# Probabilities by values in bursts of four steps instead of step by step, in a streaming encoder step with sparse attention

## Chip, cores and metric

The kernel runs on one core of a Trainium2 chip. The metric is the time of one execution on the device in microseconds (us), the median of several runs. TensorE (PE) multiplies matrices and transposes, VectorE (DVE) and ScalarE (ACT) work on vectors and empty PSUM, GpSimd (POOL) works on vectors in SBUF, and SyncE (SP) issues the DMAs.

## What is computed

One layer of a hybrid encoder over 2048 prompt tokens (with 16 meta tokens ahead of them) and 128 sample tokens. After one large input projection there are two branches, gated linear attention and sparse attention, each with its own output projection; the two are merged and projected once more. The change touches the sparse attention of the prompt: an indexer picks 256 admissible keys for each query, and 16 query heads of width 64 (4 groups of keys and values) attend over those.

```python
logits = jnp.einsum('bqgrd,bqkgd->bqgrk', qg, k_sel.astype(jnp.float32)) * DSA_SCALE
logits = jnp.where(keep[:, :, None, None, :], logits, -jnp.inf)
p = jax.nn.softmax(logits, axis=-1)
o = jnp.einsum('bqgrk,bqkgd->bqgrd', p, v_sel.astype(jnp.float32))
return o.reshape(bsz, nq, DSA_Q).astype(q.dtype)
```

The kernel does not gather: it multiplies the queries by all earlier keys and adds a mask of 0 or a very large negative number.

## The kernel before

Phase 1 makes all projections and the selection masks. Phase 2 holds the prompt's attention, with the sample tile and the linear attention as side work in its first part (query blocks 15 down to 8), and the projection `gla_project` (tile `pd`) beside it in its second (blocks 7 to 0). Phase 3 is `finish`: merge, output projection and final norm.

`attend(j)` (L998) handles a block of 128 queries against the key blocks 0 to j. It goes over two halves (8 heads each), two values of `k` (0 and 2), and two sides (two key groups). For each side:

- `logits` (L1092) loads two query heads, multiplies them by the keys into PSUM tiles `pl` (L1105, L1106; three buffers), adds the mask and takes the maximum on VectorE (L1107), reduces it (L1109), and takes the exponential on ScalarE (`act`, L154) into `lgl` and `lgu`.
- `probs` (L1040) transposes these probabilities, two key blocks of two heads per step: four transposes of 128x128 into one PSUM tile `px` (L1046; two buffers in the first part of phase 2, three in the second), and one copy to SBUF on ScalarE (L1054) or VectorE (L1056). Side 0 gives tiles `st0`, `st2`, ..., one buffer each; side 1 gives tiles `pt` from a pool of seven.
- `pv` (L1059), on side 1, multiplies a step's `st` and `pt` by the values into the PSUM tile `oo` (L1066): for each key block one product of `st` into partitions 0 to 63 and one of `pt` into partitions 64 to 127. Each is 64 columns of weights and 256 moving columns, in float32, and the trace holds two instructions for each.

The last two steps (`DEFER`) of a pair of sides wait in `self.due` and are put among the next pair's side 0 steps. The products of eight heads end with `finish_half`: the gate (`gate`, four transposes into `pl`), the meta rows (`pv_meta`: four transposes into `px`, one product into `oo`, L1077), one multiplication, and two DMAs.

The order within each engine is not the order of the code. A scheduler places instructions by their priority, the order of emission, among those that are ready in its own model of time. `early(n)` (L132) lowers the priority number by n, so that the instructions go ahead of some n earlier ones. The order is fixed when the program is built; the chip runs each engine's list in that order.

Of the kernel before, what the change touches and what calls it, by code (L numbers as in the profile page):

```python
# [37 lines left out]
NEG = -3.0e38  # L38
# [17 lines left out]
DEFER = 2  # L56
# [13 lines left out]
# Token tiles ("m" meta rows, "s" sample rows, else a prompt block) in pieces, two to a group of the  # L70
# projections; COL is a tile's first column in the scratch tensors.
# [17 lines left out]
def segments(n, most=512):  # L89
    """n split into even pieces of nearly equal width, none wider than a bank."""  # L90
    c = max(1, -(-n // most))
    w = -(-n // c)
    w += w % 2
    out, a = [], 0
    while a < n:
        out.append((a, min(w, n - a)))
        a += w
    return out


def level_masks():
    """1 where a key meets a query in the products of a chunk's levels: of a key with itself and with the
    other query of its pair; in groups of four blocks of 2, 8 and 32 tokens, of blocks 1 to 3 with the one
    before, of 2 and 3 with block 0, of 3 with block 1; the same of samples, two blocks of 8 each."""
    j = np.arange(P)[:, None]
    out = [j == np.arange(P)[None, :], j == 2 * np.arange(64)[None, :]]
    for s, blocks in (2, (0, 1, 2, 0, 0, 1)), (8, (0, 1, 2, 0, 0, 1)), (32, (0, 1, 2, 0, 0, 1)), (8, (0, -1, 2)):
        group = np.arange(P // (4 * s)).repeat(len(blocks) * s)[None, :]
        block = np.tile(np.repeat(blocks, s), P // (4 * s))[None, :]
        out.append((j // (4 * s) == group) & (j // s % 4 == block))  # L110
    return np.concatenate(out, 1).astype(np.float32)
# [6 lines left out]
class Trunk:  # L118
# [5 lines left out]
    # ---------------------------------------------------------------- helpers  # L124
    @contextmanager
    def later(self, n):
        """Instructions that yield to those of the next n or so."""
# [6 lines left out]
    def early(self, n):  # L134
        """Instructions that go ahead of the last n or so."""
# [23 lines left out]
    def split(self, hi, lo, src, scale=None):  # L159
        """src = hi + lo exactly; hi and lo are float32r."""  # L160
# [7 lines left out]
    def move(self, out, a):  # L168
        """A plain copy of float32r data."""
        self.nc.sync.dma_start(out.bitcast(F32), a.bitcast(F32))  # L170

    def ln_stats(self, pool, x, width, rows):
        """mean and 1/sqrt(var + eps) over the free axis of x[:rows, :width]."""
# [17 lines left out]
    # ---------------------------------------------------------------- scratch  # L191
# [18 lines left out]
    # ---------------------------------------------------------------- projections  # L210
    def rows_of(self, t):
        """The input rows of a token tile."""
# [6 lines left out]
    def out_rows(self, name, t, width):  # L219
        """The rows of k/v/idx_k outputs of a token tile."""  # L220
# [12 lines left out]
    def split_sb(self, hi, lo, src, eng=None):  # L233
        """split() of data in SBUF, shared by ScalarE (or VectorE) and GpSimd."""
# [3 lines left out]
    def weights(self, parts, pool=None, name="", eng=None):  # L238
        """Columns of w_in (a list of (first, count)) split in hi and lo: [128, 8, width]."""
# [19 lines left out]
    def mm3(self, ps, ah, al, bh, bl, n):  # L259
        """ps = a^T b to float32 accuracy; ah(k) ... give the operands of contraction tile k."""  # L260
# [11 lines left out]
    def prep_x(self, t, xh, xl, c, keep):  # L272
        """Transposed layer norm of a token tile, as hi and lo, and to scratch if keep names a place."""
# [20 lines left out]
    def nat(self, x, c, r, w):  # L294
        """PSUM [tokens, width] of tokens c..c+r of a piece."""
# [7 lines left out]
    def tsp(self, x, c, n, w, a):  # L303
        """PSUM [columns a..a+128 of the stripe, tokens c..c+n of a piece]."""
# [6 lines left out]
    def keys(self, t, x, c, w1, w2):  # L311
        """k, v, index keys, index weights and the low-rank gate of a token tile."""
# [26 lines left out]
        # index keys  # L339
# [15 lines left out]
    def phase_keys(self):  # L355
        """Layer norm of all tokens and everything that later tokens need of a token."""
# [48 lines left out]
    def ev_heads(self, col, ps, c, n):  # L405
        """Queries, scaled: in scratch, the lo parts of two heads follow their hi parts."""
# [23 lines left out]
    # ---------------------------------------------------------------- indexer and selection  # L430
    def index_block(self, j):
        """Scores of a prompt block against its admissible keys."""
# [62 lines left out]
    def select(self, items):  # L495
        """Masks (0 or NEG) of the top-k scores of each row, ties to the lowest key; the threshold is
        the k-th largest score, found bit by bit."""
# [49 lines left out]
    # ---------------------------------------------------------------- phase 1  # L547
# [28 lines left out]
    def project(self, g):  # L576
# [43 lines left out]
        def step(n, c):  # L620
            # ScalarE has the gates of phase 2 to do beside the last of these
            self.spare = g == len(GROUPS) - 1 and n in SPARE
            # the tiles of x that the next group takes first come free first
# [26 lines left out]
    # ---------------------------------------------------------------- gated linear attention  # L650
    def gla_gates(self):
        """Log forget gates (times 16) of all tokens, to scratch: [dk of all heads, token], in steps."""
# [25 lines left out]
    def gla_decay(self, c, r):  # L678
        """Forget gates of tokens c..c+r, [dk, head, token], and their logs' sums (times 16) after 0, 1, .. tokens."""
# [12 lines left out]
    def gla_factors(self, b, levels):  # L692
        """What the decays of a level's blocks of s tokens change by, for the next level's blocks of r * s
        tokens: of queries, of keys, and from the queries' blocks 2 and 3 to the ends of 0 and 1."""
# [22 lines left out]
    def gla_pairs(self, a, q, k, g):  # L717
        """Decays inside pairs of tokens. Returns keys decayed to the end of their pair, queries from its start."""
# [21 lines left out]
    def gla_level(self, a, k, q, s, f, level):  # L740
        """Products between the blocks of s tokens of groups of four; keys and queries of the next level."""
# [39 lines left out]
    def gla_turn(self, kt, r):  # L781
        """Keys with tokens on partitions."""
# [25 lines left out]
    def gla_out(self, c, half, po, gr, og):  # L808
        """Norm and gate of two heads' outputs (PSUM [token, 2, 256])."""
# [40 lines left out]
    def gla_chunk(self, t):  # L850
        """A chunk of 128 tokens; the state's update and the store of its outputs wait for the next one."""
# [39 lines left out]
    def gla_sample(self):  # L891
        """Linear attention of the sample tile, in steps."""
# [73 lines left out]
    # ---------------------------------------------------------------- sparse attention  # L966
    def qload(self, pool, c, h0, **kw):
        """Query heads h0 and h0 + 1, their hi and then their lo parts, on both halves of the partitions."""
# [6 lines left out]
    def gate(self, half, z, sums, nu):  # L975
        """The gates of eight heads by 1 / their sums: [(group, d), head of a group, token]."""
# [20 lines left out]
    def attend(self, j):  # L997
        """Attention of a prompt's block, in steps."""  # L998
# [10 lines left out]
        for half in range(2):  # L1009
            oo, pmeta = [], self.sm.tile([P, 4, 3, 2, META], F32, name="pmeta")  # L1010
            for k in range(0, 4, 2):
                held, steps = {}, self.steps(j)
                for side in range(2):
                    pe = self.logits(c, 4 * (2 * half + side) + k, segs, mk, ends, sums, pmeta)
                    for i, (s0, w) in enumerate(steps):
                        pt = self.probs(pe, s0, w, side)
                        if side:
                            pv = partial(self.pv, oo, half, k, s0, w, held[s0], pt)
                            if i < len(steps) - min(DEFER, len(steps) // 2):
                                pv()  # L1020
                            else:
                                self.due.append(pv)
                        else:
                            held[s0] = pt
                            if self.due:
                                self.due.pop(0)()
                    if not side:
                        self.flush()
# [11 lines left out]
    def probs(self, pe, s0, w, side):  # L1040
        """Two heads' probabilities of some key blocks, transposed."""
# [17 lines left out]
    def pv(self, oo, half, k, s0, w, t0, t1):  # L1059
        """Probabilities by values: pairs of heads of two groups side by side on the array."""  # L1060
        if not oo:
            oo.append(self.po.tile([P, 4, P], F32, name="oo"))
        for s in range(w):
            for o, t in enumerate((t0, t1)):
                d = 64 * (2 * half + o)
                self.nc.tensor.matmul(oo[0][64 * o : 64 * o + 64, k : k + 2, :], self.v[:, s0 + s, d : d + 64],  # L1066
                                      t[:, 2 * s : 2 * s + 2], start=k + s0 + s == 0, stop=False, skip_group_check=True)

    def pv_meta(self, oo, half, pmeta):
        """The meta rows' part for eight heads at once: rows (hi, hi, lo) x (group, key)."""  # L1070
# [17 lines left out]
    def steps(self, j):  # L1088
        """The key blocks of query block j by twos."""
        return [(s, min(2, j + 1 - s)) for s in range(0, j + 1, 2)]  # L1090

    def logits(self, c, h0, segs, mk, ends, sums, pmeta):  # L1092
        """exp(logits - maximum) of two heads, and their sums."""
# [23 lines left out]
    def attend_sample(self):  # L1117
        """Attention of the sample tile, in steps."""
# [7 lines left out]
        # the queries of two samples with zeros between: [q, 0] and [0, q] both lie in it  # L1126
# [77 lines left out]
    # ---------------------------------------------------------------- phase 2  # L1204
    def side_work(self):
        """Everything of phase 2 but the attention of the prompt, in steps."""
# [21 lines left out]
    def phase2(self):  # L1228
        nc, tc, d = self.nc, self.tc, self.d
        with ExitStack() as main:  # L1230
# [31 lines left out]
            # the meta rows' values of two groups at a time, block diagonal: rows (hi, lo, hi) x (group, key)  # L1262
# [43 lines left out]
    # ---------------------------------------------------------------- phase 3  # L1306
    def w3(self, pool, src, name, width, most=512, raws=None, last=None):
        """A [1024, 1024] weight, split, in blocks of some columns, one by one: [128, 8, width] each."""
# [15 lines left out]
    def x3(self, name, c0, n):  # L1324
        """Columns c0..c0+n of a transposed activation, split."""
# [8 lines left out]
    def rows3(self, name, c0, n, q):  # L1334
        """A row tile of a transposed activation."""
# [4 lines left out]
    def proj3(self, w, x, n):  # L1340
        """PSUM [128 columns of the weight, n tokens]."""
# [120 lines left out]
```

## Time and profile before

| | us |
|---|---|
| median of three runs | 3752.91 |
| lowest and highest | 3747.67, 3760.36 |
| span of the profiled execution | 3751.2 |
| TensorE busy in it | 3650.8 (97%) |
| VectorE, ScalarE, GpSimd busy | 2575.1 (69%), 1458.8 (39%), 1046.7 (28%) |
| mean granted TensorE clock | 0.984 |

The profile gives no other time for its own execution than the span, from the first to the last instruction; it is 1.7 us under the median. Busy times of TensorE are modelled at their ends, so that two neighbouring instructions can overlap in the rows by some 0.2 us; what one costs is read from start to start.

### The profile page before, as it was taken

What the parts mean: (1) busy time and instruction counts of PE and PEld (TensorE: products, weight loads), DVE (VectorE), ACT (ScalarE), POOL (GpSimd) and SP (SyncE); (2) the same over time, 40 slices, a digit from 0 to 9 for tenths busy, and PEclk for the clock granted to TensorE, in tenths of its full rate; (3) what the DMA queues carried; (4) which work ended last, traced back from release to release, by engine and by line L of the source; (5) the groups of instructions that cost most, each with busy time, mean ns of one, the idle gap of its engine ahead of it and who ended that gap; (6) DMA issues with size and microseconds to landing.
All of it is one profiled execution on the core that took longest, in us unless ns stands there. A gap on an engine that the chain in (4) does not pass through costs nothing.

```text
span 3751.2 us, 66401 instructions
## 1 busy us (share of the span) xinstructions
PE 3650.8 (97%) x24484; PEld 3255.9 (87%) x24484; DVE 2575.1 (69%) x5965; ACT 1458.8 (39%) x3084; POOL 1046.7 (28%) x1220
## 2 busy tenths in 40 slices
PE   7999999999999999999999999999999999989999
PEld 7999999999999989998986777777777788879998
DVE  7648997899999988822266777777765555554444
ACT  4444224333234233316244455555564333341110
POOL 3122343243342344344111333333320000012211
PEclk9999999999999999999899999999999999999999
DMA  8642433363432354454454232223333234564331
GB/s 262 195 118 89 144 113 95 92 172 107 132 110 87 116 172 133 120 167 132 123 149 121 68 84 79 79 80 84 85 105 101 81 101 122 140 179 149 119 117 64
DMA packets 530085, 448.82 MB, mean 120 GB/s; under 512 B 87152, under 2 KB 502000, under 8 KB 529760
## 3 DMA queue, kind: packets, MB, share of 16 engines
q1 hardware_dynamic: 529760, 444.58, 40.6%
q8 instruction: 193, 3.16, 0.3%
q14 instruction: 132, 1.08, 0.1%
HBM read 288.01 MB, written 156.44 MB: 118 GB/s over the span
## 4 chain that ended last, share of the span: by engine, by line
PE 81%; DVE 9%; DMA 5%; issue 2%; ACT 1%; POOL 1%; SPq 0%; POOLq 0%; DVEq 0%; ACTq 0%
PE pp L265 12%; PE pp L263 12%; PE pp L264 12%; PE oo L1066 9%; PE px L1046 6%; PE pd L263 3%; PE pl L1105 3%; PE pd L264 3%; PE pd L265 3%; PE pl L1106 3%; PE fo L264 1%; PE fo L263 1%; PE fo L265 1%; DVE junk L148 1%; PE pg L755 1%
## 5 line engine op out<-in xcount | busy, mean ns | idle before, releaser
L148 DVE TENSOR_SCALAR_CACHE_REDUCE junk<-sc,cand 128x272 bf16<-128x272 f32 (+6 forms) x512 | 701.8, 1371 | 17.0
L142 POOL TENSOR_TENSOR wlo<-raw,whi 128x512 fp32r<-128x512 f32 x360 | 488.6, 1378 | 795.3 <-ACT whi L157 741.0
L263 PE MATMUL pp<-xh,whi 128*128 128x384 f32 (+2 forms) x1728 | 566.6, 328 | 1.6 <-ACT whi L157 1.6
L264 PE MATMUL pp<-xl,whi 128*128 128x384 f32 (+2 forms) x1728 | 565.6, 327 | 0.0
L265 PE MATMUL pp<-xh,wlo 128*128 128x384 f32 (+2 forms) x1728 | 565.5, 328 | 0.0
L263 PE MATMUL pp<-whi,xh 128*128 128x256 f32 (+3 forms) x1952 | 561.7, 288 | 3.1 <-ACT whi L157 1.8
L265 PE MATMUL pp<-whi,xl 128*128 128x256 f32 (+3 forms) x1952 | 560.9, 288 | 3.5 <-DVE xl L142 3.5
L264 PE MATMUL pp<-wlo,xh 128*128 128x256 f32 (+3 forms) x1952 | 561.4, 288 | 0.0
L1107 DVE CUSTOM_DVE_ANT_0 lgl<-pl,mkl 128x348 f32<-128x348 f32 (+8 forms) x608 | 298.0, 511 | 134.8 <-PE pl L1106 98.8
L265 PEld LDWEIGHTS pp<-whi,xl 128*128 128x128 f32 (+1 forms) x1952 | 370.6, 190 | 13.8 <-DVE xl L142 5.6
L263 PEld LDWEIGHTS pp<-whi,xh 128*128 128x128 f32 (+1 forms) x1952 | 371.6, 190 | 11.5 <-issue 3.0
L264 PEld LDWEIGHTS pp<-wlo,xh 128*128 128x128 f32 (+1 forms) x1952 | 371.5, 190 | 5.4 <-issue 2.3
L263 PE MATMUL pd<-xh,wh 128*128 128x242 f32 (+3 forms) x1152 | 329.1, 286 | 8.8 <-ACT wh L1319 3.4
L154 ACT ACTIVATE lgl<-lgl,mx 128x1040 f32<-128x1040 f32 (+7 forms) x256 | 249.6, 975 | 213.2 <-DVE mx L1109 205.0
L263 PEld LDWEIGHTS pp<-xh,whi 128*128 128x128 f32 x1728 | 327.4, 189 | 3.3 <-ACT whi L157 2.2
L264 PEld LDWEIGHTS pp<-xl,whi 128*128 128x128 f32 x1728 | 327.4, 189 | 0.6
L265 PEld LDWEIGHTS pp<-xh,wlo 128*128 128x128 f32 x1728 | 326.8, 189 | 1.3 <-POOL wlo L142 0.7
L265 PE MATMUL pd<-xh,wl 128*128 128x242 f32 (+3 forms) x1152 | 325.6, 283 | 0.9 <-POOL wl L142 0.8
L264 PE MATMUL pd<-xl,wh 128*128 128x242 f32 (+3 forms) x1152 | 325.6, 283 | 0.0
L1105 PE MATMUL pl<-kd,q 128*128 128x348 f32 (+14 forms) x800 | 304.4, 383 | 13.6 <-DVE mx L1107 8.8
L157 ACT CAST whi<-raw 128x512 fp32r<-128x512 f32 (+1 forms) x344 | 199.1, 622 | 302.2 <-DMA raw<-in_w_in 190.9
L1066 PE MATMUL oo<-st,v 128*64 128x256 f32 x1088 | 314.5, 400 | 0.0
(250 smaller groups left out, 7666.7 us busy)
## 6 DMA issues: line engine op xcount, KB each, us to landing
raw<-in_w_in SPq DMA_DIRECT2D x360, 256.0 KB, 3.1
q<-d_q SPq DMA_DIRECT2D x272, 128.0 KB, 3.0
d_h<-x SPq DMA_DIRECT2D x17, 512.0 KB, 3.2
d_gv<-en SPq DMA_DIRECT2D x68, 128.0 KB, 2.0
d_gr<-en SPq DMA_DIRECT2D x68, 128.0 KB, 1.8
d_z<-en SPq DMA_DIRECT2D x68, 128.0 KB, 1.7
v<-d_gv SPq DMA_DIRECT2D x17, 512.0 KB, 3.7
gr<-d_gr SPq DMA_DIRECT2D x17, 512.0 KB, 3.4
```

Of the source, the lines that this page charges most:

```text
L142: (eng or self.nc.vector).tensor_tensor(out, a, b, op=op)
L148: (eng or self.nc.vector).tensor_scalar(out, a, s1, s2, op0=op0, op1=op1, **kw)
L154: self.nc.scalar.activation(out, a, f, **kw)
L157: (self.nc.vector.tensor_copy if self.spare else self.nc.scalar.copy)(out, src)
L263: mm(ps, ah(k), bh(k), start=k == 0, stop=False)
L264: mm(ps, ah(k), bl(k), start=False, stop=False)
L265: mm(ps, al(k), bh(k), start=False, stop=k == n - 1)
L1046: nc.tensor.transpose(ps[:, 2 * s + u, :], pe[u][a // KLOW][:, a % KLOW : a % KLOW + P], self.ident[:])
L1066: self.nc.tensor.matmul(oo[0][64 * o : 64 * o + 64, k : k + 2, :], self.v[:, s0 + s, d : d + 64], t[:, 2 * s : 2 * s + 2], start=k + s0 + ...
L1105: nc.tensor.matmul(ps[:, :m], q[:, u, :], kd, start=True, stop=False)
L1106: nc.tensor.matmul(ps[:, :m], q[:, 2 + u, :], kd, start=False, stop=True)
L1107: nc.vector.tensor_tensor_reduce(lg[z1][:, a : a + m], ps[:, :m], mk[z1][:, a : a + m], 1.0, NEG, OP.add, OP.max, mx[:, s : s + 1])
```

## The change

`pv` now takes a list of up to four steps (`BURST`) and issues all their products together, the newest step first and within each block side 1 (`pt`) before side 0 (`st`), at a priority raised by 3000 (`AHEAD`). The list is given to `pv` after every fourth step of side 1; what is left at the last step waits in `self.due`, and is issued, by `flush`, right after the next side 0's logits and ahead of its `probs`. The start flag of the accumulation goes to the first pair of products issued into a new `oo` tile. The count and shape of all instructions, buffers and DMAs are the same as before.

```diff
-DEFER = 2
+BURST = 4
+AHEAD = 3000
...
-                held, steps = {}, self.steps(j)
+                held, steps, burst = {}, self.steps(j), []
                 for side in range(2):
                     pe = self.logits(c, 4 * (2 * half + side) + k, segs, mk, ends, sums, pmeta)
+                    if not side:
+                        self.flush()
                     for i, (s0, w) in enumerate(steps):
                         pt = self.probs(pe, s0, w, side)
-                        if side:
-                            pv = partial(self.pv, oo, half, k, s0, w, held[s0], pt)
-                            if i < len(steps) - min(DEFER, len(steps) // 2):
-                                pv()
-                            else:
-                                self.due.append(pv)
-                        else:
+                        if not side:
                             held[s0] = pt
-                            if self.due:
-                                self.due.pop(0)()
-                    if not side:
-                        self.flush()
+                            continue
+                        burst.append((s0, w, held[s0], pt))
+                        if i == len(steps) - 1:
+                            self.due.append(partial(self.pv, oo, half, k, burst))
+                        elif len(burst) == BURST:
+                            self.pv(oo, half, k, burst)
+                            burst = []
...
-    def pv(self, oo, half, k, s0, w, t0, t1):
+    def pv(self, oo, half, k, burst):
         if not oo:
             oo.append(self.po.tile([P, 4, P], F32, name="oo"))
-        for s in range(w):
-            for o, t in enumerate((t0, t1)):
-                d = 64 * (2 * half + o)
-                self.nc.tensor.matmul(oo[0][64 * o : 64 * o + 64, k : k + 2, :], self.v[:, s0 + s, d : d + 64],
-                                      t[:, 2 * s : 2 * s + 2], start=k + s0 + s == 0, stop=False, skip_group_check=True)
+            self.fresh_bank = True
+        with self.early(AHEAD):
+            for s0, w, t0, t1 in burst[::-1]:
+                for s in range(w):
+                    for o, t in (1, t1), (0, t0):
+                        d = 64 * (2 * half + o)
+                        self.nc.tensor.matmul(oo[0][64 * o : 64 * o + 64, k : k + 2, :], self.v[:, s0 + s, d : d + 64],
+                                              t[:, 2 * s : 2 * s + 2], start=self.fresh_bank, stop=False, skip_group_check=True)
+                    self.fresh_bank = False
```

Over the whole program, the products by values stand on TensorE in 378 unbroken runs before (256 before the first product of `pd`, 122 after it) and in 106 now (63 and 43). Up to the first of these runs the order of TensorE is the same, instruction by instruction. Line numbers of the changed program differ from those before by up to five.

**TensorE, an early query block of the first part.** `oo` is written by the products by values, `pt` and `st` are side 1's and side 0's transposed probabilities, `px` is written by the transposes, `pg` belongs to the linear attention. Before:

```order
L1066 MATMUL oo<-pt,v 64x256
L1066 MATMUL oo<-st_23273,v 64x256
L1066 MATMUL oo<-pt,v 64x256
L1066 MATMUL oo<-st_23280,v 64x256
L1046 MATMUL px<-ident,lgu 128x128 x3
L1066 MATMUL oo<-pt,v 64x256
L1066 MATMUL oo<-st_23280,v 64x256
L1066 MATMUL oo<-pt,v 64x256
L1046 MATMUL px<-ident,lgu 128x128
L1066 MATMUL oo<-st_23287,v 64x256
L755 MATMUL pg<-mq,m 128x192 x2
L1046 MATMUL px<-ident,lgu 128x128 x4
```

Now, for the same two heads and the second four steps, where the run goes on for eight more products after the last row shown:

```order
L1046 MATMUL px<-ident,lgu 128x128 x8
L756 MATMUL pg<-mq,m 128x192 x2
L1078 MATMUL px<-ident,pmeta 96x128 x4
L1070 MATMUL oo<-pt,v 64x256
L1070 MATMUL oo<-st_23308,v 64x256
L1070 MATMUL oo<-pt,v 64x256
L1070 MATMUL oo<-st_23308,v 64x256
L1070 MATMUL oo<-pt,v 64x256
L1070 MATMUL oo<-st_23301,v 64x256
L1070 MATMUL oo<-pt,v 64x256
L1070 MATMUL oo<-st_23301,v 64x256
```

Before, a step's products are cut apart by transposes, and single products without a partner of the other side stand between other work; now sixteen products stand in a row, in pairs of one `pt` and one `st`, and the transposes of several steps stand next to each other.

**TensorE, the second part of phase 2, the same side in both.** Before:

```order
L1066 MATMUL oo<-pt,v 64x256
L1066 MATMUL oo<-st_31455,v 64x256
L1066 MATMUL oo<-pt,v 64x256
L1066 MATMUL oo<-st_31466,v 64x256
L1046 MATMUL px<-ident,lgl 128x128 x4
L1066 MATMUL oo<-pt,v 64x256
L1066 MATMUL oo<-st_31466,v 64x256
L1066 MATMUL oo<-pt,v 64x256
L1066 MATMUL oo<-st_31475,v 64x256
L1046 MATMUL px<-ident,lgl 128x128 x4
```

Now:

```order
L1110 MATMUL pl<-kd_20193,q 128x128
L1111 MATMUL pl<-kd_20193,q 128x128
L1046 MATMUL px<-ident,lgl 128x128 x4
L1046 MATMUL px<-ident,lgu 128x128 x2
L1046 MATMUL px<-ident,lgl 128x128 x16
L1046 MATMUL px<-ident,lgu 128x128 x2
L1070 MATMUL oo<-pt,v 64x256
L1070 MATMUL oo<-st_31482,v 64x256
L1070 MATMUL oo<-pt,v 64x256
L1070 MATMUL oo<-st_31482,v 64x256
```

Before, products stand between the transposes of one `px` tile and the next; now 24 transposes, six steps, stand in a row ahead of the run of products. It is the longest such stretch of the new program.

## Rows read from the trace of the kernel before

**Rows 1.** The page: the span, and part 1, busy time of each engine.
```profile
span 3751.2 us, 66401 instructions
PE 3650.8 (97%) x24484; PEld 3255.9 (87%) x24484; DVE 2575.1 (69%) x5965; ACT 1458.8 (39%) x3084; POOL 1046.7 (28%) x1220
```
**Rows 2.** The page, part 4: the chain that ended last, by line.
```profile
PE pp L265 12%; PE pp L263 12%; PE pp L264 12%; PE oo L1066 9%; PE px L1046 6%; PE pd L263 3%; PE pl L1105 3%; PE pd L264 3%; PE pd L265 3%; PE pl L1106 3%; PE fo L264 1%; PE fo L263 1%; PE fo L265 1%; DVE junk L148 1%; PE pg L755 1%
```
**Rows 3.** Busy time by engine in phase 2's parts: window length, engines (instructions), clock, DMA.
```profile
1917.00:2790.00 873.00, 851.88 (x5320) 636.27 (x5321) 619.15 (x2168) 466.82 (x988) 274.68 (x449) 0.99 0.30 85
2790.00:3337.00 547.00, 531.91 (x3900) 435.71 (x3898) 308.55 (x1017) 221.66 (x483) 42.50 (x150) 0.99 0.42 112
```
**Rows 4.** The same windows for L1066 alone: TensorE's products, then their weight loads.
```profile
1917.00:2790.00 873.00, 244.52 (x1450) 103.16 (x1450) 0.99 0.30 85
2790.00:3337.00 547.00, 127.84 (x726) 53.44 (x726) 0.99 0.42 112
```
**Rows 5.** TensorE's timeline, four places: start, duration, instruction, count merged.
```profile
2022.56 0.32 PE L1106 MATMUL pl<-kd,q 128*128 128x344 f32 x1
2022.81 0.43 PE L1066 MATMUL oo<-pt,v 128*64 128x256 f32 x1
...
2023.81 0.44 PE L1046 MATMUL px<-ident,lgu 128*128 128x128 f32 x2
...
2109.40 0.65 PE L1066 MATMUL oo<-pt,v 128*64 128x256 f32 x2
2109.98 0.43 PE L1105 MATMUL pl<-kd,q 128*128 128x348 f32 x1
...
2110.57 0.32 PE L1106 MATMUL pl<-kd,q 128*128 128x344 f32 x1
2110.72 0.37 PE L1105 MATMUL pl<-kd,q 128*128 128x448 f32 x1
...
2364.12 0.43 PE L1066 MATMUL oo<-pt,v 128*64 128x256 f32 x1
...
2365.99 0.66 PE L1046 MATMUL px<-ident,lgl 128*128 128x128 f32 x4
```
**Rows 6.** Timeline of products, and timeline of weight loads (PEld), at one place.
```profile
2100.67 0.43 PE L1066 MATMUL oo<-pt,v 128*64 128x256 f32 x1
...
2100.72 0.14 PEld L1066 LDWEIGHTS oo<-pt,v 128*64 128x64 f32 x1
```
**Rows 7.** Waits, 1917 to 2800 us: weight loads for another engine; total us, times, longest.
```profile
PEld pl L1105 <- DVE mx L1107: 15.9, 28, 2.3
...
PEld px L1046 <- DVE st L1056: 6.3, 5, 2.6
PEld oo L1066 <- ACT pt L1054: 3.2, 8, 0.8
...
PEld px L1046 <- ACT st L1054: 2.4, 6, 0.8
```
**Rows 8.** Groups by line and shape, 1917 to 2830 us: busy us, mean ns, idle before.
```profile
L1107 DVE CUSTOM_DVE_ANT_0 lgl<-pl,mkl 128x348 f32<-128x348 f32 x236 | 118.6, 515 | 40.6 <-PE pl L1106 29.5 <-PE px L1046 3.1 <-ACT lgu L154 2.8
L1056 DVE COPY st<-px 128x512 f32<-128x512 f32 x58 | 39.8, 686 | 14.8 <-PE px L1046 14.6
...
L154 ACT ACTIVATE lgl<-lgl,mx 128x1040 f32<-128x1040 f32 x119 | 138.3, 1163 | 73.8 <-DVE mx L1109 73.5
```
**Rows 9.** Busy time in three short windows as in rows 3, and one timeline row.
```profile
1908.00:1913.00 5.00, 5.00 (x29) 4.62 (x29) 0.35 (x1) 1.81 (x5) 0.00 (x0) 0.50 0.88 195
1919.00:1925.00 6.00, 5.90 (x44) 5.27 (x44) 5.11 (x17) 4.31 (x12) 0.00 (x0) 1.00 0.00 0
2120.00:2130.00 10.00, 6.76 (x37) 4.42 (x38) 8.06 (x29) 3.73 (x7) 3.79 (x6) 0.83 0.10 27
...
2123.68 0.66 PE L1046 MATMUL px<-ident,lgl 128*128 128x128 f32 x4 [2.40 <-DVE st L1056]
```

## Prediction

> **What bounds the kernel now.** I read the page first, then the chain of waits, then busy time by window. TensorE is busy 97% of the 3751.2 us span [rows 1], and the chain that ended last runs through TensorE's lines, with the products by values (`oo`, L1066) at 9% and the transposes into `px` at 6% [rows 2]. The change moves nothing ahead of phase 2. There TensorE is busy 851.88 of 873 us and 531.91 of 547 us, VectorE 71% and 56%, ScalarE 53% and 41% [rows 3]. So phase 2 ends when TensorE has issued its list, and a microsecond saved in that list is a microsecond of time, as long as TensorE finds its operands ready. The products by values fill 244.52 + 127.84 = 372.4 us of it [rows 4]. That is the sum the change works on.
>
> **What a run of products costs.** The timeline of TensorE tells it from start to start [rows 5].
> - A lone product (two instructions) takes 2109.40 to 2109.98 = 0.58 us until the next other instruction starts.
> - A run of two products of `pt` and one of `st` takes 2022.81 to 2023.81 = 1.00.
> - A run of seven products takes 2364.12 to 2365.99 = 1.87.
>
> These lie on one line: 0.15 us to leave a run, plus 0.43 for each slot, where a slot holds one `pt` and one `st` product side by side (they write different halves of the partitions) or one product alone. So 1, 2 and 4 slots give 0.58, 1.01 and 1.87. A product without its partner costs a full slot.
> - Entering costs too: an L1106 product of 344 columns is followed after 0.15 us by another of its kind (2110.57 to 2110.72), but after 0.25 us by a product by values (2022.56 to 2022.81). That is 0.10, so each run costs 0.25 us beside its slots.
>
> Check: the order before has 378 runs with 661 slots, so 661 x 0.43 + 378 x 0.25 = 379 us, against 372.4 busy [rows 4], which leaves out part of the entries.
>
> By the Trainium skill (TensorE: Matmul & The Clock Gate, Part 3), a weight load overlaps a running product only if the two use different rows of the array; these use the same 128 rows, so each of a slot's two loads of 0.14 us would stand alone. In this trace a load starts at 2100.72, within the product that started at 2100.67 and lasts 0.43 [rows 6], so that rule does not hold here. By it a slot would cost some 0.71, and the dropped slots below 83 us instead of 50; the sum goes by the row.
>
> **The change, term by term.**
> 1. *Fewer runs.* Counted in the order, 378 become 106. 272 x 0.25 = **68 us** saved.
> 2. *No lone products.* 1088 products fill 661 slots before; now all stand in pairs, 544 slots. 117 x 0.43 = **50 us** saved. Of the 118 us in all, 84 lie ahead of the first `pd` product and 34 behind it. No run before is longer than four slots at full clock; I take eight to be on the same line (3.6 us), since nothing between one and four bends it.
> 3. *Order inside a burst.* Newest first means that the first product waits for the newest copy and the other fifteen for nothing. This saves no time by itself; waits of products for copies cost 3.2 us today [rows 7].
> 4. *Waits that come back.* Today products by values stand between the transposes and give ScalarE and VectorE time to empty `px`. Now the transposes of several steps stand together. TensorE reuses a `px` tile after two others' turn (three in the second part), a `pl` tile after three. I added up TensorE's own work between the last write to a tile and the first write to the one that takes its place, at the durations of the rows. A copy takes 0.69 us, the masked maximum of `pl` 0.52, and an exponential of 1.16 may stand ahead on ScalarE [rows 8]. If a buffer needs 1.5 us to come back, the program before is short by 28 us in the first part. The waits seen there are 15.9 + 6.3 + 2.4 = 25 us [rows 7], so 1.5 is the need that fits. With it the shortage grows by 27 us for `px` and 13 for `pl` in the first part, and by 5 and 5 in the second: 50 us. With a need of 1.0 us it grows by 17, with 2.0 by 120.
> 5. *First products and first transposes.* With the same 1.5 us, bursts wait some 5 us more for their newest copy. From the last logits to the first transposes of the same heads the softmax takes some 3 us (0.52 + 1.16 + 1.16 and the reductions); there TensorE's work falls short by 10 us more than today, in the second part. Together 15 us. One wait lets several buffers come back, so of 50 + 15 I take **45 us** as paid. It cannot be under zero by much, since today's waits are only 25 us; the upper end is 120.
> 6. *What else moves.* The products issue no DMA. `finish_half` is emitted ahead of the next side 0's steps and not behind them; its two output DMAs on SP and its copies shift by a few us each, and their queues are far from full (ScalarE 53%, DMA 30% [rows 3]). GpSimd's queue has only the meta rows' copies of the attention, and 31% load. Nothing waits for `oo` but `finish_half`. No operation is added. I cost these at nothing; the cover is the linear attention's work, and without it a late `finish_half` holds the single `oo` bank.
> 7. *VectorE as next bound.* If the first part shrinks from 873 to some 825 us, VectorE's 619 us are 75% of it, not full.
>
> **Sum.** -68 - 50 + 45 = -73 us against the profiled span of 3751.2, so 3678; the median lies 1.7 above that span, so **3680 us**.
>
> **The rivals.**
> - *The waits do not come back* (need of 1.0 us or less). The whole gain shows: 3753 - 118 + 17 = 3652, or down to 3635. For it: today's waits are small, and the order was chosen with the copies in mind. Against: 77 of 388 `px` tiles in the first part have less than 1.5 us, against 26 of 403 today.
> - *Copies become the bound in the stretches without products* (need nearer 2 us, since VectorE rises from 71% to 75% and its requests come bunched). The gain shrinks to 10 to 45 us: 3708 to 3742.
> - *The burst starves TensorE*, the case on the other side. For 3.6 us no logits and no transposes are issued; then several tiles are asked for at once, and TensorE stands at `px` (L1046) until L1054 and L1056 have worked them off. It decides from 118 / 106 = 1.1 us of new waiting for each burst. At 1.4 us (the 120 above and 30 of lowered clock) it is 3753 - 118 + 150 = 3785. That long waits cost more than themselves is shown: a wait of 2.40 us for a copy stands in a window with clock 0.83 [rows 9]. Against: the order leaves more than 1.5 us to four tiles in five.
> - *The clock falls between bursts.* TensorE ran at 0.50 (1.2 GHz) for 5 us while busy with the sample's small products and what followed them, so being busy is not enough [rows 9]. But from 1919 to 1925 us, 30 transposes and logits, without one product by values, ran at 1.00 (2.4 GHz) [rows 9]. The longest stretch of transposes alone grows from 1.5 to 2.6 us. At 2.5 us lost for each fall, a fall after half of the bursts would cost 130 us: 3765. By the Trainium skill (TensorE: Matmul & The Clock Gate, Part 4), transposes do not count as busy for the clock, which would make this the outcome. The window at 1.00 speaks against it as far as half its time goes.
> - *The change does not do what it says*: excluded, the built order has the 106 paired runs.
>
> **Chances and range.** Forecast (a gain of 45 to 100 us) 0.58; waits stay away 0.17; copies bind 0.15, of which 0.02 end within 0.3%; burst starves 0.07, of which 0.02 within 0.3%; clock 0.03, slower. A measurement of this kernel can tell about 0.3%, 11 us, from no change. That gives faster 0.88, same 0.04, slower 0.08. The range goes from the whole gain less a few us, 3638, to a gain of 25 us, 3728. Left out are the last of the full gain (0.05), the small gains of the copies' case (0.05), and the starved and clock cases (0.10), 2 in 10.
>
> **What the next profile would show.** L1070 in place of L1066: runs of 16 products at 0.43 us a pair, start to start 3.6 us, and a sum near 260 us instead of 372 to 379. First part near 825 us, second near 525. `PEld px` and `PEld pl` waits near twice today's 25 us. Wrong if the runs cost more than a straight line says, if waits for L1054, L1056 and L1107 pass 120 us, if the granted clock falls in phase 2, or if phase 3 (unchanged) moves by more than 5 us.

## The result and the profile after

The changed kernel takes 3665.31 us (median of four runs, 3661.81 to 3667.81) against 3756.64 us for the kernel before (median of four, 3747.67 to 3762.09). The ratio is 0.9759, with a 95% interval from 0.9742 to 0.9776: 2.4% faster. The forecast was 3680 us, within 3638 to 3728. Beside the later experiments the kernel before took 3748.8 to 3751.1 us, so the gain is 84 to 91 us.

First the page of the changed kernel: its span, busy time by engine, and the chain by line. It answers to [rows 1, 2].

```profile
span 3665.3 us, 66399 instructions
PE 3534.5 (96%) x24484; PEld 3244.8 (89%) x24484; DVE 2570.0 (70%) x5965; ACT 1454.6 (40%) x3084; POOL 1050.9 (29%) x1220
...
PE pp L266 12%; PE pp L264 12%; PE pp L265 12%; PE oo L1070 6%; PE px L1046 5%; PE pd L264 3%; PE pd L265 3%; PE pd L266 3%; PE pl L1110 2%; PE pl L1111 2%; DVE lgl L1112 2%; PE fo L264 1%; PE fo L265 1%; PE fo L266 1%; DVE junk L149 1%
```

The products by values, now L1070, fall from 9% to 6% of the chain, and VectorE's masked maximum (L1112) comes into it with 2%. The span is 85.9 us shorter. TensorE's busy time fell by 116 us, so some of the gain was given back as idle time.

To see where, cut both spans at the first `pd` product and at the first `rmb`, which marks phase 3. The columns are those of [rows 3]. Before:

```profile
1917.00:2817.60 900.60, 877.40 (x5479) 654.18 (x5479) 637.62 (x2238) 487.83 (x1034) 282.41 (x460) 0.99 0.31 87
2817.60:3344.40 526.80, 512.08 (x3766) 423.06 (x3764) 293.78 (x953) 204.07 (x443) 36.05 (x139) 0.98 0.41 112
3344.40:3751.20 406.80, 393.10 (x2521) 358.11 (x2520) 188.90 (x332) 61.87 (x130) 88.56 (x96) 0.99 0.40 125
```

After:

```profile
1917.00:2751.50 834.50, 788.95 (x5305) 639.29 (x5304) 616.09 (x2169) 467.01 (x992) 284.63 (x452) 0.98 0.33 92
2751.50:3258.70 507.20, 489.76 (x3927) 432.16 (x3927) 305.02 (x1019) 218.16 (x480) 35.93 (x145) 0.99 0.44 118
3258.70:3665.30 406.60, 392.11 (x2520) 356.82 (x2520) 188.96 (x333) 61.74 (x130) 89.50 (x96) 0.99 0.41 125
```

The first part lost 66.1 us, the second 19.6, phase 3 only 0.2. In phase 2 TensorE was busy 1389.5 us and is now 1278.7, so 110.8 less. Its idle time (length less busy) grew from 37.9 to 63.0 us, by 25.1, of which 22.4 in the first part. VectorE went from 71% to 74% of the first part.

Two cautions go with these cuts. The first `pd` product does not stand at the same place of the attention in both kernels: up to it TensorE ran 5479 instructions before and 5305 now, and by the trace the missing ones are 63 transposes, 62 of the logits and 47 of the products by values, some 25 us of work at the durations of [rows 5] (an estimate), which the changed kernel does in its second part. So the split of the gain between the parts is nearer 41 and 45 than 66 and 20; the sum of the two is not touched by this. And the first logits, the same instruction of the same order, start at 1894.1 us before and at 1891.6 now, so 2.5 us of the gain in these two executions come from ahead of phase 2. Over the fourteen programs profiled for this document that start lies between 1886.4 and 1895.0, so one profile cannot settle a few microseconds of phase 2.

A run of 16 products on the timeline of TensorE in the changed kernel (start, duration, instruction):

```profile
1944.23 0.32 PE L1111 MATMUL pl<-kd,q 128*128 128x348 f32 x1
1944.48 0.43 PE L1070 MATMUL oo<-pt,v 128*64 128x256 f32 x1
1944.49 0.43 PE L1070 MATMUL oo<-st,v 128*64 128x256 f32 x1
...
1948.09 0.44 PE L1046 MATMUL px<-ident,lgl 128*128 128x128 f32 x2
```

It takes 1944.48 to 1948.09 = 3.61 us: eight slots of 0.43 and 0.15. The straight line read from runs of one to four slots [rows 5] goes on to eight. Over all, the 378 runs before took 348 us from their first product to the next other instruction, and the 106 runs now take 258; with 0.10 us for entering each run that is 117 us less.

L1070's own busy time by window, for [rows 4]:

```profile
1917.00:2724.00 807.00, 165.93 (x1376) 95.36 (x1376) 0.98 0.33 91
2724.00:3252.00 528.00, 99.52 (x800) 54.50 (x800) 0.99 0.45 118
```

265.5 us, where L1066 had 372.4. Which waits came back in the first part, here from 1917 to 2724 us (total us, times, longest), for [rows 7]:

```profile
PEld pl L1110 <- DVE mx L1112: 27.9, 35, 3.1
...
PEld oo L1070 <- DVE pt L1056: 7.2, 5, 3.0
PEld px L1046 <- ACT pt L1054: 5.6, 9, 0.9
PEld px L1046 <- DVE pt L1056: 4.8, 8, 1.8
PEld px L1046 <- ACT lgl L155: 4.1, 8, 1.6
PEld px L1046 <- DVE st L1056: 3.9, 9, 0.6
...
PEld oo L1070 <- ACT pt L1054: 2.4, 7, 0.8
...
PEld px L1046 <- ACT st L1054: 1.8, 4, 0.8
```

Three rows of the kernel before, in the window of [rows 7], that stand beside these:

```profile
PEld px L1046 <- DVE pt L1056: 0.9, 1, 0.9
...
PEld px L1046 <- ACT pt L1054: 0.7, 2, 0.4
...
PEld px L1046 <- ACT lgl L154: 0.5, 2, 0.2
```

Waits of the logits (`pl`) for VectorE grew from 15.9 to 27.9 us, those of the transposes for the copies from 10.3 to 16.1, those of the products for their newest copy from 3.2 to 9.6, and those of the transposes for the exponential from 0.5 to 4.1. The four add 28 us, about the idle time that came; they are waits of weight loads, so the two need not be equal.

### The profile page after: what moved, and what is told of

Its sections match the earlier page's. It is cut to its first block, busy times and chain, and to the rows that moved or that the text cites. A ratio compares the mean times of both kernels' runs of the same rounds, so it can differ in the third digit from the quotient of the medians.

```text
span 3665.3 us, 66399 instructions
## 1 busy us (share of the span) xinstructions
PE 3534.5 (96%) x24484; PEld 3244.8 (89%) x24484; DVE 2570.0 (70%) x5965; ACT 1454.6 (40%) x3084; POOL 1050.9 (29%) x1220
## 4 chain that ended last, share of the span: by engine, by line
PE 75%; DVE 13%; DMA 5%; ACT 2%; issue 2%; POOL 1%; SPq 0%; POOLq 0%; DVEq 0%; ACTq 0%
PE pp L266 12%; PE pp L264 12%; PE pp L265 12%; PE oo L1070 6%; PE px L1046 5%; PE pd L264 3%; PE pd L265 3%; PE pd L266 3%; PE pl L1110 2%; PE pl L1111 2%; DVE lgl L1112 2%; PE fo L264 1%; PE fo L265 1%; PE fo L266 1%; DVE junk L149 1%
## 5 line engine op out<-in xcount | busy, mean ns | idle before, releaser
L1112 DVE CUSTOM_DVE_ANT_0 lgl<-pl,mkl 128x348 f32<-128x348 f32 (+8 forms) x608 | 297.1, 510 | 84.4 <-PE pl L1111 52.9
L1118 POOL COPY pmeta<-lgl 128x48 f32<-128x48 f32 x256 | 58.8, 230 | 766.0 <-ACT lgl L155 761.1
```

Source lines behind the costliest of these rows:

```text
L1112: nc.vector.tensor_tensor_reduce(lg[z1][:, a : a + m], ps[:, :m], mk[z1][:, a : a + m], 1.0, NEG, OP.add, OP.max, mx[:, s : s + 1])
```

## The experiments

Two numbers are counted in the order of each kernel: runs of products by values, and slots. The kernel before has 378 and 661, the changed one 106 and 544. Each ratio below is to the kernel before, measured beside the experiment, with its 95% interval.

**1. The raised priority alone.**

```diff
-        for s in range(w):
-            for o, t in enumerate((t0, t1)):
...
+        with self.early(3000):
+            for s in range(w):
+                for o, t in enumerate((t0, t1)):
...
```

> The kernel before with one thing changed: the products of a step are issued at the priority raised by 3000; still step by step, oldest first, side 0 before side 1. In the order TensorE has 309 runs with 604 slots (changed kernel 106 and 544, kernel before 378 and 661). Theory (time follows runs at 0.25 us and slots at 0.43 us, and waits of TensorE shrink as runs are added, by some 0.1 us for each run): 3665 + 203 x 0.25 + 60 x 0.43 - 20 = 3722 us, between 3712 and 3742. Rival (the raised priority is what helps, because probabilities are used and their buffers come free sooner): 3665 to 3685 us.

Measured: 3720.33 us, ratio 0.9918 (0.9898 to 0.9937). The theory gave 3722. The priority alone brings a third of the gain, by way of 69 runs and 57 slots less than before. The rival falls.

**2. Bursts without the priority.**

```diff
-AHEAD = 3000
+AHEAD = 0
```

> The changed kernel with AHEAD = 0: bursts of four steps, newest first, at no raised priority. In the order TensorE has 360 runs with 668 slots. Theory (runs and slots): 3665 + 254 x 0.25 + 124 x 0.43 - 25 = 3757 us, as slow as the kernel before, between 3740 and 3785. Rival (issuing bursts in the code is what helps, whatever the scheduler makes of them): 3665 to 3690 us.

Measured: 3783.16 us, ratio 1.0085 (1.0066 to 1.0105): slower than the kernel before, within the theory's range but 26 us over its number. Phase 2 of its profile (window length, then TensorE busy):

```profile
1917.00:3369.70 1452.70, 1396.09 (x9219) 1086.49 (x9219) 921.67 (x3185) 684.61 (x1470) 320.15 (x598) 0.99 0.34 93
```

TensorE is as busy as before (1396.1 against 1389.5 us) and idle 56.6 us against 37.9. The scheduler cuts the bursts into 360 runs, so nothing is saved, and waits come on top; that it is the products' later place that brings them was not traced. Writing bursts in the code is worth nothing unless they stand as bursts in the order.

**3. Pairs without bursts.**

```diff
-BURST = 4
+BURST = 1
```

> The changed kernel with BURST = 1: the products of one step at a time, side 1's first, raised priority. In the order TensorE has 250 runs with 544 slots, so all products stand in pairs, but in 2.4 times as many runs as in the changed kernel. Theory (runs and slots): 3665 + 144 x 0.25 - 14 = 3687 us, between 3678 and 3701: the pairs alone bring most of the gain. Rival (only long runs pay, the pairs do nothing): near the kernel before less its 128 runs' worth, 3725 us or more.

Measured: 3672.22 us, ratio 0.9793 (0.9773 to 0.9813). That is 7 us over the changed kernel, where the theory had 22. The rival falls: pairs without bursts bring most of the gain. By the counts that is 50 us for 117 slots and 32 us for the 128 runs that this order has less than the kernel before, so it does not price the pairs alone. Phase 2 tells why bursts add so little:

```profile
1917.00:3266.40 1349.40, 1305.20 (x9232) 1054.90 (x9230) 918.04 (x3188) 684.57 (x1473) 317.67 (x597) 0.98 0.37 103
```

TensorE is busy 26.5 us longer than in the changed kernel, but idle 44.2 us and not 63.0. The 144 runs that bursts of four save cost some 19 us of waits.

**4. Bursts without pairs.** All products of side 1, then all of side 0.

```diff
-            for s0, w, t0, t1 in burst[::-1]:
-                for s in range(w):
-                    for o, t in (1, t1), (0, t0):
...
+            for o in (1, 0):
...
+                for s0, w, t0, t1 in burst[::-1]:
+                    for s in range(w):
...
```

> The changed kernel with the products inside a burst in another order: first all of side 1 (into partitions 64 to 127), then all of side 0 (into partitions 0 to 63). Same 106 runs, 992 slots where 544 were, since only the two at the seam of the sides can stand side by side. Theory (a product without a partner of the other side beside it costs a whole slot): 3665 + 448 x 0.43 = 3858 us, less up to 30 us of waits that the longer runs hide, 3825 to 3865. Rival (the array overlaps products of the two sides wherever they stand in the run, or the order inside the run is of no account): 3665 us.

Measured: 3812.87 us, ratio 1.0163 (1.0142 to 1.0184). Pairs are shown to matter, by 148 us, but the number was 45 us over. The timeline of one such run says why:

```profile
1932.70 3.02 PE L1071 MATMUL oo<-pt,v 128*64 128x256 f32 x13
1935.35 0.43 PE L1071 MATMUL oo<-st,v 128*64 128x256 f32 x1
1935.56 0.38 PE L1071 MATMUL oo<-pt,v 128*64 128x256 f32 x1
1935.62 0.38 PE L1071 MATMUL oo<-st,v 128*64 128x256 f32 x1
1935.77 0.38 PE L1071 MATMUL oo<-pt,v 128*64 128x256 f32 x1
1935.83 0.38 PE L1071 MATMUL oo<-st,v 128*64 128x256 f32 x1
1935.99 0.38 PE L1071 MATMUL oo<-pt,v 128*64 128x256 f32 x1
1936.05 2.97 PE L1071 MATMUL oo<-st,v 128*64 128x256 f32 x13
1938.95 0.66 PE L1046 MATMUL px<-ident,lgu 128*128 128x128 f32 x4
```

The run takes 6.25 us, 14.2 slots and not 15: the first `st` product starts while three instructions of `pt` that stand ahead of it in the list have not started. So the seam hides two products, not one. All 35 runs of eight and eight take 14.2 slots, those of four and four 6.1, those of one and one 1.0. In the order 96 of the 106 runs have a seam, and 8 of these are a single pair, so 88 x 2 + 8 = 184 products are hidden: 1088 - 184 = 904 slots make 3665 + 360 x 0.43 = 3820 us, 7 us over what was measured.

**5. Bursts of four, oldest step first.**

```diff
-            for s0, w, t0, t1 in burst[::-1]:
+            for s0, w, t0, t1 in burst:
```

> The changed kernel with the steps of a burst issued oldest first instead of newest first; raised priority and side 1 before side 0 within a block as in the changed kernel. In the order TensorE has 250 runs with 544 slots, the same counts as with bursts of one step: the first product no longer waits for the newest copy, so the scheduler starts each burst early and cuts it. Theory (only runs, slots and waits count): as bursts of one step, 3672 us, between 3664 and 3682. Rival (newest first has a worth of its own, one wait for a copy in place of four): 3690 us or more.

Measured: 3679.53 us, ratio 0.9807 (0.9792 to 0.9822). The order is as cut as with bursts of one step (250 runs), and so is the time, 7 us apart, about what can be told. So newest first works by making the burst hold together. Its worth is that of the runs it saves less the waits they bring: 14 us, where 144 runs are 36.

**6. Bursts of two.**

```diff
-BURST = 4
+BURST = 2
```

> The changed kernel with BURST = 2. In the order TensorE has 161 runs with 544 slots. What is left of the span beside slots and runs (other work and waits) was 3397 us with bursts of four and 3372 with bursts of one, so long bursts bring waits back. Theory (a middle length takes most of the saving for half of the waits): 544 x 0.43 + 161 x 0.25 = 274, plus 3382, plus 2 outside the span: 3658 us, between 3648 and 3668. Rival (the waits come from the raised priority and the pairs, not from the length of the run): 274 + 3397 + 2 = 3673 us.

Measured: 3668.35 us, ratio 0.9778 (0.9763 to 0.9792), at the theory's upper bound, and no difference to bursts of four that can be measured. The time does not tell the two readings apart, the less so as 3397 and 3372 rest on run times from the traces (269 and 300 us) and 274 on the counts; with the 281 us that this trace shows, the two would be 3665 and 3680. TensorE's idle time in phase 2 speaks for the theory: 44 us with bursts of one, 57 with two, 63 with four.

**7. The copies of the first part on ScalarE.**

```diff
-TURNS = "DAA", "DDA"
+TURNS = "A", "DDA"
```

> The changed kernel with all copies of the first part of phase 2 on ScalarE (VectorE had one in three). Order: 96 runs, 544 slots. Theory (the waits that came back, some 32 us, are VectorE's: it holds both the copies of px and the masked maxima of pl, and in the first part TensorE's waits for L1112 grew from 16 to 28 us): VectorE loses some 80 us of work in the first part, half of these waits go, 3648 us, between 3640 and 3657. Rival (a tile is missed for the time of one copy, whoever makes it, or ScalarE with its exponentials of 1.16 us is the worse place): 3662 to 3690 us.

Measured: 3640.94 us, ratio 0.9704 (0.969 to 0.9719), 24 us better than the changed kernel. Waits from 1917 to 2724 us, as above:

```profile
PEld pl L1110 <- DVE mx L1112: 19.7, 24, 2.2
...
PEld px L1046 <- ACT pt L1054: 10.6, 10, 2.9
...
PEld px L1046 <- ACT st L1054: 6.8, 10, 2.4
PEld oo L1070 <- ACT pt L1054: 5.9, 12, 1.4
```

`pl` waits 8 us less; `px`, now for ScalarE alone, waits about as long as before (17.4 against 16.1), and the products 4 us less. Waits for VectorE went, as the theory said. Experiment 9 asks whether they were the burst's.

**8. A PSUM bank from the logits to the transposes.**

```diff
-PLB = 3
+PLB = 2
...
-PXB = 2
+PXB = 3
```

> The changed kernel with one PSUM bank moved from the logits (pl, three to two) to the transposes (px, two to three in the first part of phase 2, four in the second). Order: 90 runs, 544 slots, worth 4 us less than in the changed kernel. Theory (the waits that came back are for the turn of px, since it is the transposes that now stand together): 3650 us, between 3642 and 3659. Rival (they are for pl, whose products wait for VectorE's L1112): 3675 us or more.

Measured: 3699.66 us, ratio 0.9863 (0.9846 to 0.9879). Theory wrong, rival right:

```profile
PEld pl L1110 <- DVE mx L1112: 42.4, 63, 3.0
```

With two `pl` banks the logits wait 42.4 us in the same window, against 27.9. The third `pl` bank is worth more than a third for `px`.

**9. The same copies in the kernel before**, as a control for 7.

```diff
-TURNS = "DAA", "DDA"
+TURNS = "A", "DDA"
```

> The kernel before with all copies of the first part of phase 2 on ScalarE (as in the run that brought the changed kernel to 3641 us). Order: 374 runs, 653 slots, worth 4 us less than before. Theory (what the copies on VectorE cost is mostly the waits that the bursts brought; the kernel before has few): 3751 - 4 = 3747 us, between 3738 and 3756, so the gain of the copies is the changed kernel's alone. Rival (VectorE is in the way of either kernel alike): the same 24 us, 3727 us or less.

Measured: 3733.11 us, ratio 0.9954 (0.9942 to 0.9967), 18 us under the kernel before. Both readings miss. Some 4 us are the runs and slots it has less. So by the medians most of what 7 gained is not the burst's waits: 18 of the 24 us are to be had without the change. Its phase 2:

```profile
1917.00:3325.50 1408.50, 1375.96 (x9209) 1066.75 (x9206) 848.29 (x3042) 752.63 (x1600) 317.09 (x597) 0.99 0.35 97
```

TensorE is idle for 32.5 us, 5.4 less than before. With these copies the change is worth 3733 - 3641 = 92 us, without them 84 to 91, so by the medians the two about add up. The profiles say otherwise. From the first logits to the first `rmb` the copies gave 12.9 us in the kernel before (1450.4 to 1437.5) and 27.9 in the changed one (1367.1 to 1339.2), because in this execution the same instructions ahead of the first logits took 6.0 us less than in the kernel before, and in that of experiment 7 they took 3.4 more than in the changed kernel. How much of the 24 us goes with the change, 6 or 15, stays open.

**10. Bursts of two with these copies.**

```diff
-TURNS = "DAA", "DDA"
+TURNS = "A", "DDA"
...
-BURST = 4
+BURST = 2
```

> The changed kernel with BURST = 2 and all copies of the first part on ScalarE. Order: 155 runs, 544 slots, 59 runs and 15 us more than bursts of four with these copies (3641 us). Theory (with VectorE relieved the long burst has few waits left to save, and the runs decide): 3650 us, between 3644 and 3658. Rival (a shorter burst still saves as many waits as its runs cost, as it did with the copies on both engines): 3641 us or less.

Measured: 3648.77 us, ratio 0.9737 (0.9722 to 0.9752), the theory's 3650. With VectorE relieved the longer burst is worth 8 us, which experiment 6 could not show, but not the whole 15 us of its 59 runs: from the first logits to the first `rmb` TensorE is busy 14 us longer than in experiment 7 (1297.2 against 1283.1) and idle 5 less (50.8 against 56.2).

**11. More copies on ScalarE in the second part.**

```diff
-TURNS = "DAA", "DDA"
+TURNS = "A", "DA"
```

> The changed kernel with all copies of the first part on ScalarE, and in the second part one in two instead of one in three on ScalarE. Order: 94 runs, 544 slots. Theory (VectorE is under 60% busy in the second part, three px buffers are there, and few waits came back in it): no difference to the copies of the first part alone, 3641 us, between 3633 and 3647. Rival (the stretches of 24 transposes wait for VectorE's two copies in three): 3630 us or less.

Measured: 3639.02 us, ratio 0.9699 (0.9686 to 0.9712): no difference to 7, as the theory said. Experiments 7 and 11 are the best versions found, faster than both kernels.

**12. Bursts of six with these copies.**

```diff
-TURNS = "DAA", "DDA"
+TURNS = "A", "DDA"
...
-BURST = 4
+BURST = 6
```

> The changed kernel with BURST = 6 and all copies of the first part on ScalarE; seven buffers of side 1's probabilities as before. Order: 80 runs, 544 slots, 16 runs and 4 us less than bursts of four with these copies. Theory (longer runs save 0.25 us each and bring back as much in waits): 3641 us, between 3634 and 3650. Rival (the runs decide alone): 3636 us; (six tiles of seven held by one burst, so that the next side's copies stand still): 3655 us or more.

Measured: 3655.87 us, ratio 0.9751 (0.9737 to 0.9764), 15 us worse than bursts of four, as the last rival had it, but mostly not where it said. In the waits of ScalarE and VectorE over phase 2:

```profile
ACT st L1054 <- PE oo L1070: 30.7, 12, 5.3
...
DVE st L1056 <- PE oo L1070: 16.0, 9, 4.5
...
DVE pt L143 <- PE oo L1070: 8.2, 2, 5.0
```

In experiment 7 the first two are 3.9 and 4.1 us, and the third is not there. It is mostly side 0's tiles `st0`, `st2`, ..., with one buffer each, that the long burst holds; the next side 0's copies stand at them. Side 1's pool of seven, which I had named, shows in the third row alone: the gate's tile comes out of that pool and waited twice. From the first logits to the first `rmb` TensorE is idle for 65.8 us, 9.6 more than in experiment 7; that these copies are what it waited for is likely but was not tried, and phase 3, which took 6 us more in this execution, is not explained.

## Why the prediction was right

**What bounds the kernel.** Phase 2 ends with TensorE's list: 110.8 us less of TensorE's work, with 25.1 us more idle, gave 85.7 us of phase 2, of which 2.5 us are the earlier start. Phase 3 did not move.

**Runs and slots** (terms 1 and 2, 118 us). Held: 117 us from start to start. The straight line holds from one to eight slots (3.61 us), and experiments 1, 4 and 10 came out by it, 1 and 10 with a few us allowed for waits, 4 within 7 us once the seam is counted right. Experiments 3 and 4 show the two parts: pairs without bursts 3672, bursts without pairs 3813.

**Newest first** (term 3). Held: nothing by itself (experiment 5), but it is what keeps the scheduler from cutting the burst. The forecast called that a matter of waits; it is a matter of order.

**Waits that come back** (terms 4 and 5, 45 us). This is the term that was mis-sized: 25 us of idle time came. By its parts, in the first part of phase 2: `pl` 13 forecast, 12.0 measured; newest copies 5 forecast, 6.4 measured; `px` 27 forecast, 5.8 measured. So `px` is the part that was mis-sized. Of the softmax's 10 us in the second part little is seen: idle time there grew from 14.7 to 17.4 us, though waits for the exponential grew by 3.6 us in the first part, where none were forecast. The need of 1.5 us was fitted to `pl` and `px` together, and only the share of `pl` came out by it; why `px` came back with less no run shows. The forecast of 48 us for the first part and the 66 measured cannot be set against each other, since the two cuts hold different work. Of 118 - 25 = 93 us, 86 show in the profile. Most of the other 7 can be the clock, which the sum put at nothing: summed from the trace, TensorE stood at the lower of its two levels for 48 us of phase 2, where it was 38 before, and 10 us more at half the clock cost some 5 (an estimate). That loss made up part of the 20 us by which the waits came out smaller, so it is in part luck that the forecast of 3680 came as near as 15 us.

**What else moves, and VectorE** (terms 6 and 7). Held: `finish_half` shows no new wait, VectorE has 74% of the first part where 75% was forecast.

**The rivals.** Waits did come back. Copies did not become the bound. TensorE was not starved, though the waits are longest at VectorE's work; experiment 8 took a bank from `pl` and lost 34 us, which shows where that case would begin. The clock did not fall for the transposes: the new stretch of 24, which with its waits took 5.6 us and not the 2.6 of the forecast, ran in the window below at clock 1.00 (the columns are those of [rows 3]). It did fall more often elsewhere, which the forecast had named as a sign of being wrong: in the first part TensorE stood at the lower level for 41 us, where it was 21 before (in the second for 7, where it was 17). All the stretches at the lower level in the first part but the earliest stand beside waits of TensorE of 0.8 to 2.8 us. That is what the starved case counted on, though net of the second part it cost some 5 us and not its 30.

```profile
2817.70:2823.30 5.60, 4.22 (x26) 2.59 (x26) 2.74 (x10) 4.50 (x11) 0.45 (x2) 1.00 0.33 89
```

The Trainium skill (TensorE: Matmul & The Clock Gate, Part 4) says that the full clock does not engage for transposes. Here 5.6 us of transposes alone, with waits of 0.2 to 0.4 us between them, ran at the full clock, and the next fall came only at 3250 us, so the rule cost this stretch nothing; whether transposes alone would raise a lowered clock no run shows.

## What to carry to other kernels

Products that use half of the array's columns should stand next to a partner of the other half, and their runs should be long: each lone product cost a full 0.43 us slot and each change from full to half columns and back 0.25 us, which the timeline shows from start to start and busy percentages do not. With a scheduler in between, look at the order it makes: a burst in the code became one only with a raised priority and with the product first that is ready last. A longer run then pays little, since the waits that it brings take back much of what its fewer runs save (8 us of 15 were left from two steps to four in experiment 10, and no difference could be measured in 6), and it loses once it holds buffers that other engines need, which here was at six steps.

## What the runs showed that was not expected

- Products of `st`, into partitions 0 to 63, started ahead of three instructions of `pt`, into partitions 64 to 127, that stand before them in TensorE's list (experiment 4: `st` at 1935.35, `pt` at 1935.56, 1935.77 and 1935.99), at full overlap, so that two products on each side of a seam run side by side.
- Moving VectorE's third of the first part's copies to ScalarE gained 18 us in the kernel before (experiment 9). VectorE was busy 71% of that part [rows 3], and the named waits of TensorE for VectorE in its first part come to some 22 us in all [rows 7]; TensorE's idle time fell by 5.4 us only. In the profiled execution 6.0 us of the gain lie ahead of the first logits, where the two orders are the same, and TensorE stood at the lower clock level for 21 us of phase 2, where it was 38 before; what of these comes with the copies no run separates.
- One long wait costs more than itself. In the changed kernel, in the window below, TensorE waited 2.56 us for a copy, and the granted clock of the 10 us is 0.77.

```profile
2347.00:2357.00 10.00, 7.20 (x43) 4.93 (x43) 8.02 (x30) 3.88 (x8) 4.95 (x8) 0.77 0.22 54
```

The product that waited, on TensorE's timeline:

```profile
2353.07 0.69 PE L1070 MATMUL oo<-pt,v 128*64 128x256 f32 x1 [2.56 <-DVE pt L1056]
```
